# Token mixing of an encoder layer: two heads of a direction in one tile, gates first, a hand-written order of steps

## The chip, the cores and the metric

The kernel runs on one core of a Trainium2 chip. Its engines are PE (TensorE, matrix products; PEld is its weight load), DVE (VectorE), ACT (ScalarE), POOL (GpSimd) and SP (SyncE, which issues the loads here). Each takes its own instructions in order and waits for the others through semaphores. The metric is the device time of one execution in microseconds (us); lower is better.

## What is computed

```python
def rms_norm(x, g):
    return x * rsqrt(mean(x * x, -1) + EPS) * g

def swiglu(h, w_gate, w_up, w_down):
    return (silu(h @ w_gate) * (h @ w_up)) @ w_down

def gla_chunked(q, k, v, g):              # a head: dk 64, dv 128; 8 chunks of 64 tokens
    bcum = cumsum(g within the chunk);  b_last = its last row
    q_in, k_in = q * exp(bcum), k * exp(-bcum)
    att = tril(q_in @ k_in.T);  o_intra = att @ v
    k_st = k * exp(b_last - bcum);  d_state = k_st.T @ v
    state[n + 1] = exp(b_last[n]) * state[n] + d_state[n]
    return o_intra + q_in @ state

def token_mixing(h):                      # q k v r z_fwd z_bwd | Bg Cg xv = h @ w_in
    g = log_sigmoid(z @ w2 + b2) / 16     # per direction, rank 16
    o = gla(q / 8, k, v, g_fwd) + flip(gla(flip(q / 8), flip(k), flip(v), flip(g_bwd)))
    a = rms_norm(o per head, gla_norm) * silu(r)
    c = Bg * conv3(Cg * xv)
    return concat([a, c]) @ w_out

x = x + 0.5 * swiglu(rms_norm(x, ffn1_norm), ...)
x = x + token_mixing(rms_norm(x, mix_norm))
x = x + cross_attention(rms_norm(x, xattn_norm), rms_norm(mem, mem_norm))   # 4 heads, 256 memory tokens
x = x + 0.5 * swiglu(rms_norm(x, ffn2_norm), ...)
out = rms_norm(x, final_norm)             # 512 tokens, model width 1024, feed-forward width 2816
```

All is float32. The kernel makes each large product out of three products of a rounded part and a remainder.

## The kernel before

Activations lie transposed, 128 channels on the partitions and 512 tokens on the free axis; `x` and its two parts `xs` have eight such tiles. A weight unit is a slab of 128 x 1024 that SP loads into `raw` (L59), ACT rounds into `whi` (L65) and DVE completes with `wlo`, the remainder (L66). `mm3` (L68 to L73) makes three products of it on PE: whi with the high part of x (L69), whi with the low part (L70), wlo with the high part (L71). A unit of columns is 24 such products of 512 columns (`mm_cols`). Four raw buffers and three each of whi and wlo are in flight.

Four stages follow each other: the first feed-forward half step, token mixing, cross attention, the second half step with the last norm. The stage that changes is token mixing. The Tile framework orders the instructions of each engine by the code, its priorities and a cost model; on the chip every engine's order is then fixed. Small products that belong to sums over tokens wait in a list (`pend`) and go in one at a time after each `mm3` (`tick`).

Token mixing of before goes like this. `vps` takes v in two parts, part 0 (256 columns) and then part 1 (256 columns of v, and the 32 of z); the norm's factor goes to the tokens (`tok`) and, by `spread` (L145), to rows. `qk` projects q and k, 128 channels for two heads at a time, and copies each head's 64 rows to both halves of a tile (L410, L411): a head's tile has the forward direction in rows 0 to 63 and the backward one in rows 64 to 127. The gates come after q: four products of z, then log-sigmoid by `Abs`, `Exp`, `Ln` on ACT with `mn` on DVE and a subtraction on POOL (L443). `gate(h)` sums them per chunk by two scans of 64 x 512, one per direction (L449, L450), and makes `kin`, `qin`, `kst` and the decay.

`gla(h)` is a head in five steps: (1) four transposes of kst into `tp`, copied to `kn` by ACT (L482); (2) 16 products `dS` and 12 updates of the state S on DVE (L506, L508), a direction at a time in 64 rows; (3) eight products `ap`, and `att` made from them by two masked copies `put` and an addition `both` (L518, L524); (4) `ops`, four products with att and eight with S and qin, and o, its squares `osq` (L537, L539); (5) sums of the squares `rt_o`, and `spread`, which gives the head's output its factor (L545). `spread` makes two diagonal tiles `dg` on DVE (L162) and two products `sp_o` with ones on PE (L164). `rstd_tok` has the 1/rms: `ms` on DVE (L138), the root on POOL (L139). `gla_out` takes silu(r) on POOL.

Round the heads stand the units of the convolution, of `silu_r` and of the memory. `conv(j)` has three units, c, x and b (`cps`, `xps`, `bps`). The memory is split with its gain (`mem_split`), its squares are added on POOL (`mssq`), its factor is spread as `sp_mem` and multiplied into each key tile when it leaves PSUM; `mem_keys` has eight units (`mkps`), `mem_values` eight more. The order of these is a planner's: `skewed` starts a head four steps after the one before, and a loop over the units takes one step of a head after each unit.

## Time and profile before

| | before |
|---|---|
| time, median of 3 runs | 1152.45 us (1152.05 to 1152.57) |
| the profiled execution, its span | 1150.4 us |
| PE busy, of the span | 1118.1 us, 97% |
| DVE, ACT, POOL busy | 50%, 34%, 15% |
| token mixing, 370.77 to 618.29 | 247.52 us, PE busy 226.83 |
| granted clock of PE in it | 0.94 |

The profile is one execution of the program. Busy time counts matrix products on PE; register and semaphore instructions and the issue of loads don't count. The granted clock is a share of full speed. In a timeline row the first number is the start in us from the start of the span, the second the time that the instruction (or the xN merged ones) took, then engine, line, operation, output<-inputs and shape; in brackets is the idle time before it and what ended it.

### The profile page before, as it was taken

How to read it: one execution, taken by the hardware profiler on the slowest of the kernel's cores; microseconds unless marked ns; L12 is line 12 of the kernel's file. 1: busy time of each engine (PE TensorE's matmuls, PEld its weight loads, DVE VectorE, ACT ScalarE, POOL GpSimd, SP SyncE). 2: the span in 40 equal slices, each digit the busy share in tenths (PEclk: the TensorE clock that was granted, in tenths of full speed). 3: DMA queues.
4: the chain of work that ended last, by engine and by line, in shares of the span. 5: the costliest groups of instructions: out<-in, count | busy, mean ns of one | idle time of the engine just before them, and what ended most of it. 6: DMA issues, size and time to landing. Idle time of an engine off the chain costs nothing.

```text
span 1150.4 us, 13140 instructions
## 1 busy us (share of the span) xinstructions
PE 1118.1 (97%) x5326; PEld 934.3 (81%) x5326; DVE 576.9 (50%) x735; ACT 392.0 (34%) x549; POOL 173.9 (15%) x145
## 2 busy tenths in 40 slices
PE   8999999999999997798999999999999999999997
PEld 6888888888888986687887888888888888888886
DVE  6455455442333459855767445464555455442223
ACT  6332332322223284322334344353332332232221
POOL 4111111010111027211111300031111011000110
PEclk9999999999999999999999999999999999999998
DMA  6322222323333312311333322032222322323312
GB/s 218 113 95 98 100 92 94 106 85 101 101 95 124 109 56 64 101 56 57 128 104 117 105 79 74 19 128 92 92 92 93 109 92 92 105 83 101 101 51 74
DMA packets 34252, 109.08 MB, mean 95 GB/s; under 512 B 4080, under 2 KB 7152, under 8 KB 34192
## 3 DMA queue, kind: packets, MB, share of 16 engines
q1 hardware_dynamic: 34048, 108.23, 28.8%
q8 instruction: 41, 0.67, 0.2%
q14 instruction: 19, 0.16, 0.0%
q10 hardware_dynamic: 144, 0.02, 0.0%
HBM read 106.14 MB, written 2.10 MB: 94 GB/s over the span
## 4 chain that ended last, share of the span: by engine, by line
PE 86%; DVE 7%; issue 3%; ACT 1%; POOL 1%; DMA 1%; SPq 0%; POOLq 0%; DVEq 0%; ACTq 0%
PE pg_b L69 4%; PE pg_b L71 3%; PE pd_a L69 3%; PE pu_b L71 3%; PE pu_b L69 3%; PE pg_b L70 3%; PE pd_a L71 3%; PE pd_a L70 3%; PE pu_b L70 3%; PE pu_a L71 3%; PE pu_a L70 3%; PE pu_a L69 3%; PE pg_a L69 3%; PE pg_a L70 3%; PE pg_a L71 3%
## 5 line engine op out<-in xcount | busy, mean ns | idle before, releaser
L71 PE MATMUL pu_a<-xh,wlo_ua 128*128 128x512 f32 x176 | 68.7, 390 | 1.3 <-DVE wlo_ua L66 1.3
L71 PE MATMUL pg_a<-xh,wlo_ga 128*128 128x512 f32 x176 | 68.7, 391 | 0.6 <-DVE wlo_ga L66 0.6
L69 PE MATMUL pg_a<-xh,whi_ga 128*128 128x512 f32 x176 | 69.2, 395 | 0.0
L70 PE MATMUL pg_a<-xl,whi_ga 128*128 128x512 f32 x176 | 68.9, 392 | 0.1
L69 PE MATMUL pg_b<-xh,whi_gb 128*128 128x512 f32 x176 | 68.8, 391 | 0.0
L69 PE MATMUL pu_a<-xh,whi_ua 128*128 128x512 f32 x176 | 68.6, 390 | 0.0
L70 PE MATMUL pg_b<-xl,whi_gb 128*128 128x512 f32 x176 | 68.5, 389 | 0.0
L70 PE MATMUL pu_a<-xl,whi_ua 128*128 128x512 f32 x176 | 68.5, 389 | 0.0
L71 PE MATMUL pg_b<-xh,wlo_gb 128*128 128x512 f32 x176 | 68.5, 389 | 0.0
L71 PE MATMUL pu_b<-xh,wlo_ub 128*128 128x512 f32 x176 | 68.5, 389 | 0.0
L69 PE MATMUL pd_a<-hh_a,whi_da 128*128 128x512 f32 x176 | 68.5, 389 | 0.0
L70 PE MATMUL pd_a<-hl_a,whi_da 128*128 128x512 f32 x176 | 68.5, 389 | 0.0
L71 PE MATMUL pd_a<-hh_a,wlo_da 128*128 128x512 f32 x176 | 68.5, 389 | 0.0
L69 PE MATMUL pu_b<-xh,whi_ub 128*128 128x512 f32 x176 | 68.5, 389 | 0.0
L70 PE MATMUL pu_b<-xl,whi_ub 128*128 128x512 f32 x176 | 68.5, 389 | 0.0
L69 PE MATMUL pd_b<-hh_b,whi_db 128*128 128x512 f32 x154 | 59.9, 389 | 0.0
L70 PE MATMUL pd_b<-hl_b,whi_db 128*128 128x512 f32 x154 | 59.9, 389 | 0.0
L71 PE MATMUL pd_b<-hh_b,wlo_db 128*128 128x512 f32 x154 | 59.9, 389 | 0.0
L235 POOL TENSOR_TENSOR fh_a<-fs_a,fb_a 128x512 f32<-128x512 f32 x22 | 30.8, 1402 | 186.5 <-DVE fb_a L233 155.6
L235 POOL TENSOR_TENSOR fh_b<-fs_b,fb_b 128x512 f32<-128x512 f32 x22 | 28.4, 1292 | 198.9 <-DVE fb_b L233 182.2
L66 DVE TENSOR_TENSOR wlo_db<-raw_db,whi_db 128x896 fp32r<-128x896 f32 (+1 forms) x24 | 29.3, 1220 | 54.8 <-ACT whi_db L65 54.2
L66 DVE TENSOR_TENSOR wlo_da<-raw_da,whi_da 128x896 fp32r<-128x896 f32 (+1 forms) x24 | 28.4, 1182 | 49.8 <-ACT whi_da L65 49.1
(361 smaller groups left out, 2773.3 us busy)
## 6 DMA issues: line engine op xcount, KB each, us to landing
raw_gb<-in_w2gu SPq DMA_DIRECT2D x22, 512.0 KB, 3.5
raw_ub<-in_w2gu SPq DMA_DIRECT2D x22, 512.0 KB, 3.4
raw_ga<-in_w1gu SPq DMA_DIRECT2D x21, 512.0 KB, 3.5
raw_ua<-in_w1gu SPq DMA_DIRECT2D x21, 512.0 KB, 3.4
raw_da<-in_w1d SPq DMA_DIRECT2D x16, 448.0 KB, 3.3
raw_db<-in_w2d SPq DMA_DIRECT2D x16, 448.0 KB, 3.2
raw_da<-in_w1d SPq DMA_DIRECT2D x8, 512.0 KB, 3.5
raw_wk<-in_wk SPq DMA_DIRECT2D x8, 512.0 KB, 3.6
```

The lines of the kernel that those rows point to most:

```text
L66: nc.vector.tensor_tensor(lo[:, c], raw[:, c], hi[:, c].bitcast(F32), ALU.subtract)
L69: nc.tensor.matmul(ps, lhsT=whi, rhs=xhi, start=start, stop=False)
L70: nc.tensor.matmul(ps, lhsT=whi, rhs=xlo, start=False, stop=False)
L71: nc.tensor.matmul(ps, lhsT=wlo, rhs=xhi, start=False, stop=stop)
L235: nc.gpsimd.tensor_tensor(h, s, b, ALU.mult)
```

## The change

Two heads of one direction now share a tile of 128 rows: rows 0 to 63 belong to head 2j, rows 64 to 127 to head 2j + 1, and the tiles are named (r, j) for direction r and pair j. A projection of q or k leaves PSUM as it is, without copies. A scan, a state update, a subtraction now work on 128 rows of one direction: four scans of 128 x 512 in place of eight of 64 x 512, 24 updates of 128 x 128 in place of 48 of 64 x 128. The products of a head can't be shared: dS has 16 for a tile, each with weights of 64 rows and 64 columns, S has 32 for a pair, each with 64 rows.

The order of the first part is: v part 1 with z, q0, q1 with the gates in the middle, k0, k1, the gate of tile (0, 0), v part 0, the gate of (1, 0). The subtraction after `Ln` and the product with kst go to DVE, that of qin to POOL. The convolution's factor goes to cv on POOL before the last unit. The memory's squares come as four tiles of 512 columns added on DVE; its factor is spread before the splits and multiplied in with the gain, so that keys and values leave PSUM by a split alone. The steps of `gla(0)` and `gla(1)`, the convolutions, r and the keys are called one after another in a list written out by hand.

```diff
+    gbias = const.tile([P, 2 * NP], F32, name="gbias")
+    for r in DIRS:
+        for hh in range(2):
+            nc.sync.dma_start(gbias[hh * 64:(hh + 1) * 64, r * NP:(r + 1) * NP],
+                              t["headc"][r * 64:(r + 1) * 64, hh:H:2])
     gatew = big("gatew")[0:32, :]
-    nc.sync.dma_start(gatew, t["gatew"])
+    for r in DIRS:
+        nc.sync.dma_start(gatew[:, r * NP * P:(r + 1) * NP * P].rearrange("p (h c) -> p h c", c=64),
+                          t["gatew"].rearrange("p (h r c) -> p r h c", r=2, c=64)[:, r])
...
+    vz(1, 4, nmix.tok)
+    rtok = nmix.r
...
+    def qk(dst, key, j, sc, between=None):
+        ps = bank(f"{key}ps{j}")
+        w = unit(win[key][j], D, f"w{key}{j}")
+        mm_cols(ps, w, xs, ALL[:4], True, False)
+        if between:
+            between()
+        mm_cols(ps, w, xs, ALL[4:], False, True)
+        nc.vector.scalar_tensor_tensor(dst[j], ps, sc, rstd, ALU.mult, ALU.mult)
...
+    GT = [(r, j) for j in range(NP) for r in DIRS]
+    lgs, ts, lns = {}, {}, []
+    def gates():
+        for r, j in GT:
+            ps = bank(f"gps{r}{j}")
+            n = r * NP + j
+            c = slice(n * P, (n + 1) * P)
+            mm3(ps, gh[:, c], gl[:, c], zh, zl, True, True)
...
+        for g in GT:
+            nc.vector.tensor_tensor(lgs[g], lgs[g], ts[g], ALU.subtract)
...
+    qk(q2, "q", 0, 0.125, turn_z)
+    qk(q2, "q", 1, 0.125, gates)
+    qin, kin, kst, dec = {}, {}, {}, {}
+    def gate(r, j):
+        bc, lg = ts[r, j], lgs[r, j]
+        if r == 0:
+            nc.vector.tensor_tensor_scan(bc, rst[0], lg, 0.0, ALU.mult, ALU.add)
+        else:
+            nc.vector.tensor_tensor_scan(bc[:, ::-1], rst[1][:, ::-1], lg[:, ::-1], 0.0, ALU.mult, ALU.add)
...
+        nc.vector.tensor_tensor(lg, k2[j], lg, ALU.mult)
+        kst[r, j] = lg
+        nc.gpsimd.tensor_tensor(bc, k2[j], bc, ALU.mult)
+        kin[r, j] = bc
+        nc.gpsimd.tensor_tensor(e1, q2[j], e1, ALU.mult)
+        qin[r, j] = e1
...
+    qk(k2, "k", 0, 1.0)
+    qk(k2, "k", 1, 1.0)
+    gate(0, 0)
+    vz(0)
...
+    gate(1, 0)
...
-        s = tmp.tile([P, T], F32, tag="fb", name=f"{key}s{j}")
-        nc.vector.scalar_tensor_tensor(s, ps, sc, rstd, ALU.mult, ALU.mult)
-        for hh in range(2):
-            src = s[hh * 64:(hh + 1) * 64, :]
-            nc.scalar.copy(dst[2 * j + hh][0:64, :], src)
-            nc.scalar.copy(dst[2 * j + hh][64:128, :], src)
...
-        nc.gpsimd.tensor_tensor(lgs[h], lgs[h], ts[h], ALU.subtract)
...
-        nc.gpsimd.tensor_tensor(df, k2[h], df, ALU.mult)
-        kst.append(df)
-        nc.vector.tensor_tensor(q2[h], q2[h], e1, ALU.mult)
-        qin.append(q2[h])
-        nc.gpsimd.tensor_tensor(k2[h], k2[h], bc, ALU.mult)
...
-        for n in range(NCH):
-            r = slice((n % 2) * 64, (n % 2) * 64 + 64)
-            nc.tensor.matmul(dS[n % 2][:, (n // 2) * P:(n // 2 + 1) * P],
-                             lhsT=kn[r, (n // 2) * P:(n // 2 + 1) * P], rhs=v[n // 2][r, h * P:(h + 1) * P],
-                             start=(n < 2), stop=(n >= NCH - 2), skip_group_check=True)
...
-        for s in range(1, NCH - 1):
-            nc.vector.scalar_tensor_tensor(S(FW, s + 1), S(FW, s), dec[h][FW, s:s + 1], ds(FW, s), ALU.mult, ALU.add)
-            n = NCH - 1 - s
-            nc.vector.scalar_tensor_tensor(S(BW, n - 1), S(BW, n), dec[h][BW, n:n + 1], ds(BW, n), ALU.mult, ALU.add)
...
+            order = list(range(NCH)) if r == 0 else list(range(NCH))[::-1]
...
+            for n in order:
+                tk = ROWS[n % 2]
+                for hh in range(2):
+                    h = 2 * j + hh
+                    nc.tensor.matmul(dS[n % 2][ROWS[hh], (n // 2) * P:(n // 2 + 1) * P],
+                                     lhsT=kn[tk, (n // 2) * P + hh * 64:(n // 2) * P + (hh + 1) * 64],
+                                     rhs=v[n // 2][tk, h * P:(h + 1) * P],
+                                     start=n in order[:2], stop=n in order[-2:], skip_group_check=True)
...
+            for a, b in zip(order[1:], order[2:]):
+                nc.vector.scalar_tensor_tensor(S(r, full, b), S(r, full, a), dec[r, j][:, a:a + 1], ds(a),
+                                               ALU.mult, ALU.add)
...
-            nc.tensor.matmul(ops[:, c], lhsT=S(slice(0, P), n), rhs=qin[h][:, c],
-                             start=False, stop=(n == NCH - 1), skip_group_check=True)
...
+            for r in DIRS:
+                for hh in range(2):
+                    nc.tensor.matmul(ops[hh][:, c], lhsT=S(r, ROWS[hh], n), rhs=qin[r, j][ROWS[hh], c],
+                                     start=False, stop=(n == NCH - 1 and r == 1), skip_group_check=True)
...
+            nc.gpsimd.tensor_tensor(os[hh], os[hh], sr[2 * j + hh], ALU.mult)
+        for hh in range(2):
+            h = 2 * j + hh
+            ps = spread(rs[hh], 4, f"o{h}")
+            nc.vector.scalar_tensor_tensor(os[hh], os[hh], headc[:, H + h:H + h + 1], ps, ALU.mult, ALU.mult)
+            ah, al = big(f"ah{h}", F32R), big(f"al{h}", F32R)
+            split(os[hh], ah, al)
...
+        nc.gpsimd.tensor_tensor(cv, cv, rstd, ALU.mult)
...
-        nc.gpsimd.tensor_tensor(cv, bs, cv, ALU.mult)
+        nc.vector.tensor_tensor(bs, bps, cv, ALU.mult)
...
+    def mem_squares():
+        mssq = big("mssq")
+        nc.scalar.activation(mssq, mraw[0], AF.Square)
+        for i in range(1, KD // 2):
+            sq = tmp.tile([P, T], F32, tag="sq", name=f"msq{i}", bufs=2)
+            nc.scalar.activation(sq, mraw[i], AF.Square)
+            nc.vector.tensor_tensor(mssq, mssq, sq, ALU.add)
+        r_, todo = rstd_tok([mssq[:, 0:NM], mssq[:, NM:2 * NM]], 2, D, "mem")
+        for part in todo:
+            pend.extend(part)
+        mem["r"] = r_
+    def mem_rows():
+        mem["rows"] = big("mr")[:, 0:NM]
+        nc.scalar.copy(mem["rows"], spread(mem["r"], 2, "mem"))
...
+        f = tmp.tile([P, T], F32, tag="fa", name=f"mf{d}")[:, 0:NM]
+        nc.vector.scalar_tensor_tensor(f, raw, gains[:, GMEM, d:d + 1], mem["rows"], ALU.mult, ALU.mult)
+        m2 = big(f"mem{d}", F32R)
+        split(f, m2[:, 0:NM], m2[:, NM:2 * NM])
...
-            nc.vector.tensor_tensor(kf, ps[:, 0:NM], mr, ALU.mult)
             m2 = big(f"mk{n}", F32R)
-            split(kf, m2[:, 0:NM], m2[:, NM:2 * NM])
+            evict_split(ps[:, 0:NM], m2[:, 0:NM], m2[:, NM:2 * NM])
...
-    steps = skewed([gla(h) for h in range(H)], 4)
-    convs = chain(conv(j) for j in range(4))
-    for d in range(4):
-        next(convs)
-        gate(d)
-        mem_split(d)
...
+    g0, g1 = gla(0), gla(1)
+    cv = chain(conv(j) for j in range(4))
+    rr, kk = silu_r(), mem_keys()
+    next(cv)
+    next(g0)
+    next(cv)
+    next(g0)
+    gate(0, 1)
+    next(g0)
+    next(cv)
+    next(g0)
+    gate(1, 1)
+    next(cv)
+    next(g0)
+    mem_squares()
+    next(cv)
+    next(g0)
+    mem_rows()
+    next(cv)
+    for h in range(H):
+        next(rr)
+        if h == 0:
+            next(g1)
+        if h == 1:
+            next(g1)
+            next(g1)
+        if h == 2:
+            next(g1)
+        mem_split(2 * h)
+        mem_split(2 * h + 1)
+    next(g0)
+    next(kk)
+    next(g1)
+    next(kk)
+    next(g0)
+    next(g0)
+    next(kk)
+    next(g1)
+    next(cv)
+    next(g1)
+    next(cv)
+    next(cv)
+    next(g1)
+    next(g1)
+    for _ in cv:
         pass
-    for h in range(ndone, H):
-        gla_out(h)
+    for _ in kk:
+        pass
+    for _ in mem_values():
+        pass
```

On PE, the first dS block of before: each product has 128 columns of weights for a head of both directions, and neighbouring products read different halves of the rows (the two banks dS_3394 and dS_3395).

```order
L496 MATMUL dS_3394<-v_2849,kn_3342 128x128
L496 MATMUL dS_3395<-v_2849,kn_3342 128x128
L496 MATMUL dS_3394<-v_2850,kn_3342 128x128
L496 MATMUL dS_3395<-v_2850,kn_3342 128x128
L496 MATMUL dS_3394<-v_2851,kn_3342 128x128
L496 MATMUL dS_3395<-v_2851,kn_3342 128x128
```

And of after, tile (0, 0): x2 are the two heads of a chunk, 64 x 64 weights each.

```order
L511 MATMUL dS_3167<-v_2733,kn_3124 64x128 x2
L511 MATMUL dS_3168<-v_2733,kn_3124 64x128 x2
L511 MATMUL dS_3167<-v_2734,kn_3124 64x128 x2
L511 MATMUL dS_3168<-v_2734,kn_3124 64x128 x2
L511 MATMUL dS_3167<-v_2735,kn_3124 64x128 x2
L511 MATMUL dS_3168<-v_2735,kn_3124 64x128 x2
```

Where a head's chunk gave one product of 128 columns, two of 64 now follow each other on the same 64 rows of kn and v.

PE at the first spread of a head's output, before; xps and bps are convolution units.

```order
L70 MATMUL xps_3630<-xl_126,whi_wx_3632 128x512
L71 MATMUL xps_3630<-xh_125,wlo_wx_3633 128x512
L164 MATMUL sp_o_3667<-dg_o_3672,onesr 128x512
L164 MATMUL sp_o_3667<-dg_o_3675,onesr 128x512
L69 MATMUL bps_3679<-xh_111,whi_wb_3681 128x512
L70 MATMUL bps_3679<-xl_112,whi_wb_3681 128x512
```

And after; mkps are units of the memory's keys, sp_o_3883 and sp_o_3899 the factors of heads 0 and 1.

```order
L70 MATMUL mkps_3843<-mem_3760,whi_wk_3845 128x256
L71 MATMUL mkps_3843<-mem_3760,wlo_wk_3846 128x256
L164 MATMUL sp_o_3883<-dg_o_3888,onesr 128x512
L164 MATMUL sp_o_3883<-dg_o_3891,onesr 128x512
L164 MATMUL sp_o_3899<-dg_o_3904,onesr 128x512
L164 MATMUL sp_o_3899<-dg_o_3907,onesr 128x512
L69 MATMUL mkps_3915<-mem_3560,whi_wk_3917 128x256
L70 MATMUL mkps_3915<-mem_3560,whi_wk_3917 128x256
```

Two spreads now follow one another, with no unit between them.

DVE at that place, before: the work for sp_o_3667 with what stands ahead of it.

```order
L580 TENSOR_TENSOR bs_3568<-bps_3537,rstd_nmix 128x512
L66 TENSOR_TENSOR wlo_wb_3682<-raw_wb_3680,whi_wb_3681 128x1024
L120 TENSOR_TENSOR cl_3572<-cv_3510,ch_3571 128x512
L138 TENSOR_SCALAR ms_o_3603<-rt_o_3575 128x4
L158 CAST rh_o_3668<-r_o_3576 128x4
L159 TENSOR_TENSOR rl_o_3669<-r_o_3576,rh_o_3668 128x4
L162 TENSOR_TENSOR dg_o_3672<-ident,rh_o_3668 128x512
L162 TENSOR_TENSOR dg_o_3675<-ident,rl_o_3669 128x512
```

DVE after, from the output that needs sp_o_3883 to the second diagonal tile of sp_o_3899.

```order
L582 SCALAR_TENSOR_TENSOR o_3457<-o_3457,headc,sp_o_3883 128x512
L66 TENSOR_TENSOR wlo_wx_4039<-raw_wx_4037,whi_wx_4038 128x1024
L539 COPY_PREDICATED att_3837<-mf,both_3840 128x512
L648 TENSOR_TENSOR mk_3878<-mkps_3843,mk_3878 128x256
L120 TENSOR_TENSOR al_3896<-o_3457,ah_3895 128x512
L158 CAST rh_o_3900<-r_o_3766 128x4
L159 TENSOR_TENSOR rl_o_3901<-r_o_3766,rh_o_3900 128x4
L162 TENSOR_TENSOR dg_o_3904<-ident,rh_o_3900 128x512
L162 TENSOR_TENSOR dg_o_3907<-ident,rl_o_3901 128x512
```

Before, the rounding and both diagonal tiles stood behind one split of weights and one remainder; after, the second spread's stand behind an output that itself waits for the first spread, a split of weights, a masked copy and two remainders.

DVE at the sums of the memory's squares, after (before, they were POOL's).

```order
L596 TENSOR_TENSOR cs_3321<-cps_3290,rstd_3084 128x512
L66 TENSOR_TENSOR wlo_wr_3516<-raw_wr_3514,whi_wr_3515 128x1024
L539 COPY_PREDICATED att_3343<-mb,ap_3324 128x512
L545 TENSOR_TENSOR both_3346<-ap_3323,att_3343 128x512
L539 COPY_PREDICATED att_3349<-mb,ap_3326 128x512
L539 COPY_PREDICATED att_3343<-mf,both_3346 128x512
L545 TENSOR_TENSOR both_3352<-ap_3325,att_3349 128x512
L626 TENSOR_TENSOR mssq<-mssq,msq_3357 128x512
L539 COPY_PREDICATED att_3349<-mf,both_3352 128x512
L626 TENSOR_TENSOR mssq<-mssq,msq_3360 128x512
L626 TENSOR_TENSOR mssq<-mssq,msq_3363 128x512
```

The last of the three additions to mssq stands behind the four masked copies and the two additions of the first pair.

## Rows read from the trace of the kernel before

**Rows 1.** The page, part 1: span, and busy time of each engine.

```profile
span 1150.4 us, 13140 instructions
PE 1118.1 (97%) x5326; PEld 934.3 (81%) x5326; DVE 576.9 (50%) x735; ACT 392.0 (34%) x549; POOL 173.9 (15%) x145
```

**Rows 2.** Windows: length, busy PE, PEld, DVE, ACT, POOL, clock, DMA, GB/s.

```profile
370.77:618.29 247.52, 226.83 (x1272) 194.06 (x1271) 161.34 (x249) 95.87 (x141) 52.33 (x45) 0.94 0.27 86
```

**Rows 3.** Timeline of PE, token mixing: waits.

```profile
450.47 0.79 PE L71 MATMUL xps<-xh,wlo_wx 128*128 128x512 f32 x1 [3.58 <-DVE wlo_wx L66]
...
465.15 1.16 PE L496 MATMUL dS<-v,kn 64*128 64x128 f32 x16 [1.75 <-ACT kn L482]
...
484.54 2.04 PE L530 MATMUL ops<-att,v 128*128 128x128 f32 x8 [5.54 <-DVE att L518]
...
527.02 0.38 PE L164 MATMUL sp_mem<-dg_mem,onesr 128*128 128x256 f32 x1 [2.84 <-DVE dg_mem L162]
...
570.12 0.55 PE L530 MATMUL ops<-att,v 128*128 128x128 f32 x1 [2.73 <-DVE att L518]
...
616.84 0.47 PE L164 MATMUL sp_o<-dg_o,onesr 128*128 128x512 f32 x1 [0.72 <-DVE dg_o L162]
```

**Rows 4.** Windows with the lower clock (columns as in rows 2).

```profile
450.04:453.45 3.41, 2.98 (x7) 2.40 (x8) 3.35 (x4) 0.21 (x1) 1.51 (x1) 0.50 0.49 153
484.17:494.41 10.24, 9.87 (x35) 8.92 (x36) 4.42 (x7) 1.81 (x3) 0.00 (x0) 0.50 0.20 68
528.55:531.96 3.41, 3.15 (x9) 2.03 (x8) 2.33 (x4) 0.37 (x1) 0.70 (x1) 0.50 0.50 154
569.51:579.75 10.24, 9.63 (x45) 9.66 (x46) 3.26 (x6) 1.10 (x3) 0.00 (x0) 0.50 0.34 104
```

**Rows 5.** Timeline of PE at full clock: small products between large ones.

```profile
472.16 1.16 PE L514 MATMUL ap<-q,k 64*128 64x128 f32 x16
473.25 0.50 PE L69 MATMUL xps<-xh,whi_wx 128*128 128x512 f32 x1
473.59 0.39 PE L70 MATMUL xps<-xl,whi_wx 128*128 128x512 f32 x1
473.82 0.40 PE L71 MATMUL xps<-xh,wlo_wx 128*128 128x512 f32 x1
...
535.70 1.90 PE L534 MATMUL ops<-q,S 128*128 128x64 f32 x16
537.41 0.48 PE L69 MATMUL rps<-xh,whi_wr 128*128 128x512 f32 x1
```

**Rows 6.** Timeline of DVE, the gate stretch.

```profile
424.08 2.30 DVE L449 TENSOR_TENSOR_SCAN ta<-rst,mn 64x512 f32<-64x512 f32 x1 [5.00 <-POOL mn L443]
...
431.65 1.22 DVE L449 TENSOR_TENSOR_SCAN ta<-rst,mn 64x512 f32<-64x512 f32 x1
...
437.90 2.14 DVE L66 TENSOR_TENSOR wlo_wc<-raw_wc,whi_wc 128x1024 fp32r<-128x1024 f32 x1
```

**Rows 7.** Timelines of ACT and POOL, the gate stretch.

```profile
410.55 0.62 ACT L411 COPY q<-qs 64x512 f32<-64x512 f32 x1
...
411.90 1.28 ACT L436 ACT_TABLE_LOAD   x1
...
422.76 6.90 POOL L443 TENSOR_TENSOR mn<-mn,ta 128x512 f32<-128x512 f32 x4 [36.63 <-ACT ta L438]
```

**Rows 8.** Timeline of DVE: splits, masked copies, and a spread.

```profile
480.79 1.22 DVE L66 TENSOR_TENSOR wlo_wc<-raw_wc,whi_wc 128x1024 fp32r<-128x1024 f32 x1
481.92 0.72 DVE L518 COPY_PREDICATED att<-mb,ap 128x512 f32<-128x512 int32 x1
482.67 0.69 DVE L524 TENSOR_TENSOR both<-ap,att 128x512 f32<-128x512 f32 x1
...
614.44 0.16 DVE L138 TENSOR_SCALAR ms_o<-rt_o 128x4 f32<-128x4 f32 x1 [1.18 <-PE rt_o L133]
615.73 0.17 DVE L158 CAST rh_o<-r_o 128x4 fp32r<-128x4 f32 x1 [1.13 <-POOL r_o L139]
```

More of the change, by code (lines that the diff above doesn't have):

```diff
@@ L522, in gla @@
[L522 to L531 removed]
+            for r in DIRS:
+                for hh in range(2):
+                    nc.tensor.matmul(aps[hh][r][:, c], lhsT=kin[r, j][ROWS[hh], c], rhs=qin[r, j][ROWS[hh], c],
+                                     start=(i == 0), stop=(i == 3), skip_group_check=True)
```

288 lines of the change are left out of this document (119 added, 169 removed).

## The prediction, made before the changed kernel ran

> **What bounds the kernel now.** I read the busy shares first: PE is busy for 97% of the span [rows 1], so only three things can move the time: PE's idle time, the clock it is granted, and the number and price of its instructions. The change touches token mixing alone, so the second view is that stage cut out of the span: 247.52 us long, PE busy in 226.83 of them, clock 0.94 [rows 2]. PE thus stands idle for 247.52 - 226.83 = 20.7 us. The third view is PE's timeline, in which an idle time stands in brackets with what ended it. The reader is to see that PE always waits for a short chain on DVE or ACT: 3.58 us for the low half of a weight unit, 1.75 for kn, 5.54 and 2.73 for att, 2.84 for the diagonal tile of the memory's factor [rows 3]. After such a wait PE often runs on at half the clock (0.50, the lower of its two levels, 1.2 GHz): 3.41 us of it after the waits of 3.58 and 2.84, 10.24 us after those of 5.54 and 2.73 [rows 3, 4]. In these four stretches PE is busy for 2.98 + 9.87 + 3.15 + 9.63 = 25.6 us; at the full clock that is half, so the low clock costs 12.8 us. A perfect stage would win 20.7 + 12.8 = 33.5 us.
>
> **The change, part by part.** The account of time is that of the profiled execution: 1150.4 us of span, and the median of the runs shown is 2.1 us longer, which I add at the end.
>
> *The gate stretch.* Before, PE waits for weights because DVE is late: its first scan starts at 424.08 after an idle 5.00 us [rows 6], behind four subtractions on POOL that take 6.90 us [rows 7]; then eight scans, 1.22 us each alone and 2.30 beside POOL, and a weight split stretched to 2.14 us, stand before the units that PE wants [rows 6]. The change orders v with z first, makes the gates during q1, and gives the subtractions to DVE. Between the gates and the first convolution unit PE now has k0, k1 and the other part of v: 24 + 24 products of 0.23 us (473.59 to 473.82) [rows 5] and 96 half as wide, an estimate of 22.4 us. Walking the stage from 370.8 with these prices, the gate products end near 395.7. ACT then needs two table loads of 1.28 and, up to the first logarithm, six operations of about 0.62 [rows 7]: 402.9 with a little queueing. From there to the weights of the first convolution unit DVE has four subtractions, q and k of a pair, a weight split, four scans, small copies, three more operations of 512 columns, and the split itself; 512 columns take 0.69 and a split 1.22, and each overlaps the next by 0.08 (480.79 to 481.92) [rows 8]: 2.4 + 1.2 + 1.1 + 4.6 + 0.5 + 1.8 + 1.1 = 12.7, so 415.6, and PE wants them at 421.0. The next split follows 4.8 later, at 420.4, wanted at 426.9. POOL works beside it for four multiplications, which is 6.9 us by the like count of rows 7; if DVE runs at 1.22/2.14 of its pace for all of that [rows 6, 8], it loses 3.0. The slack of 5.4 and 6.5 covers it. So the waits for weights and for kn go (a unit of 24 products now lies between the transposes and dS); if the cover fails, PE waits 3 us or so and the clock falls.
>
> *Waits for att and for the memory's factor.* ops of the first pair now come a whole convolution unit after ap, 24 x 0.23 = 5.5 us, and those of the second pair after three key units; the memory's factor is spread well before its use. All the old waits are taken away: **-20.7**, and their low clock **-12.8**.
>
> *New waits.* (1) The row sums of the memory's squares stand behind DVE's work on att: from the end of unit c1, DVE does cs, one weight split, four masked copies (0.72 less the overlap), two additions (0.69) [rows 8] and three additions of squares, 0.2 + 0.6 + 1.1 + 2.6 + 1.2 + 1.8 = 7.5, while PE has ap and x1, 1.1 + 5.5 = 6.6. PE waits **1.0** (0.6 to 1.5). (2) Two spreads in a row, before mkps_3915. Before, each spread stood alone and cost at most 0.72 [rows 3]. Now the second one's diagonal tile is made behind everything in DVE's excerpt. From the end of the last r unit DVE has eight operations of 0.60, four masked copies of 0.65, three weight splits of 1.13, six of 256 columns (0.38, an estimate), some tiny ones, and the 1.3 us between ms_o at 614.44 and rh_o at 615.73, in which POOL takes the root [rows 8]: 4.8 + 2.6 + 3.4 + 2.3 + 0.5 + 1.3 = 14.9. PE meanwhile has two key units, the 16 ap products and the first spread: 5.8 + 1.1 + 0.5, some 1.5 for switches between kinds of products and small sums, and some 2 because the last key tile of memory is only split 4.8 after the start: 11.0. It waits 3.9, and 0.5 more for the second tile: **4.4**. The weight split standing among these rows waits for nothing; queued behind the wait on DVE is only the next head's output. (3) The last spread pair: the second diagonal tile comes behind bs, o (which waits for the first spread), a weight split and cl. From the end of the bps unit: 0.2 + 0.6 + 0.6 + 1.1 + 0.6 + 0.6 = 3.7, plus 0.2 until PE sees it, less the 0.5 of the first spread: **3.4**. Together 8.8; for the range 6 to 11, since neighbours on DVE's queue can shift by one or two operations.
>
> *Clock after them.* A wait of 2.84 was followed by 3.41 us at half clock, one of 2.73 by 10.24 [rows 3, 4]; that costs 3.0/2 = 1.5 or 9.8/2 = 4.9. I cannot tell which, and take the middle for both: **+6.4** (from 0 to 9.8).
>
> *Work on PE.* dS becomes 128 products instead of 64, each with 64 rows and 64 columns of weights; the trace shows none such. The nearest is ap, 64 rows by 128 columns in alternating row groups: 16 in 1.09 us (472.16 to 473.25), 0.068 each [rows 5]. If the two heads' products lie fully side by side, the 128 take the time of the old 64: +0. If each goes alone at the price of S, 16 in 1.71 (535.70 to 537.41), 0.107 [rows 5], it is 13.7 - 4.4 = +9.3. I take 0.068, as the form is nearest to ap: +4.4. S becomes 128 of 64 rows in alternating groups instead of 64 of 128 rows (6.8 us): between +0 and 128 x 0.107 - 6.8 = +6.9; at ap's 0.068 it is 8.7, +1.9. Two more sums for the memory, 0.1. Work: **+6.4** (0 to 16.3). In the new dS order the two heads of one chunk, issued next to each other, use the same 64 rows, and only chunks alternate. The Trainium skill, TensorE: Matmul & The Clock Gate, Part 3: Packing small matmuls, says that a weight load overlaps a running product only where the row group differs; by it half of the dS products would cost 0.107, 64 x 0.039 = 2.5 us more, 1143.1 in all. The ap rows, where groups alternate each time, can't decide that.
>
> *At nothing:* the 16 copies that leave ACT (ACT is half idle in the stage); fewer scans and state updates on DVE beyond what the walk counts; normalizing the memory first and evicting directly; the convolution's product shifted to DVE, hidden behind the next unit's 5.5 us; the added small loads of gate biases at the start. Were DVE short again, they would show in the waits above.
>
> **Sum:** -20.7 - 12.8 + 8.8 + 6.4 + 6.4 = -11.9. Span 1150.4 - 11.9 = 1138.5, time 1138.5 + 2.1 = 1140.6.
>
> **The rivals.** *Better:* the half clock doesn't follow the new waits as long (-4), and dS and S cost little (-5): about 1131. For it: in the stage the wait of 1.75 shows no fall, so short waits may be free [rows 3, 4]. Against it: 2.73 and 2.84 did bring one.
> *DVE late in the gate stretch:* POOL's multiplications slow the scans as before, the slack is eaten, PE waits 3 and runs slow for 1.5: about 1145. For it: 2.30 against 1.22 for a scan [rows 6]. Against: a slack of 5.4 and more.
> *The packed products go one after another:* dS and S at 0.107, +16.2 instead of +6.3: 1150.5, within 0.2% of before. For it: 64 x 64 is a form that the trace doesn't have. Against: ap runs 64-row products in pairs already.
> *Slower:* each of these products also pays for a switch. After ap the first large product takes 0.34 (473.25 to 473.59) where others take 0.23 [rows 5], 0.11 for a change of form; if two neighbours on different parts of the array pay it between them, a product costs 0.107 + 0.05 = 0.157, and 256 of them 256 x (0.157 - 0.068) = 22.8 more: 1163.4. It decides from 0.068 + 14.2/256 = 0.123 each. Against: ap changes groups at every product and pays nothing. The Trainium skill, TensorEngine Tiling (Array Packing), Key Properties, says that a change of tiling mode drains the engine and a change of tile alone does not; by that this rival is wrong inside a block, and ap agrees.
> *It doesn't do what it says:* the order brings a wait as long as those removed at another place, 1152.
>
> **How the numbers follow.** Forecast, 1134 to 1147: 0.55. Better: 0.21. DVE late: 0.09. Packed one by one: 0.07. Slower: 0.05. Nothing gained: 0.03. The likeliest is 1140.6. The range is 1129 (no half clock and cheap products, 1140.6 - 6.4 - 5) to 1150.5 (the serial case); outside it lie the slower case, the case of nothing gained, and half of the serial one and some of the better one, under 0.2. A measurement of this kernel can tell about 0.2%, 2.3 us, from no change. Faster by more: 0.55 + 0.21 + 0.09 + a little of the serial case = 0.87. Same: 0.07. Slower: 0.06.
>
> **What would show it.** In the profile after: PE idle in the stage of some 9 us instead of 20.7; no wait for wlo of the convolution or for att; waits of 3 to 5 us before the second of two neighbouring spreads; clock above 0.94; 16 dS products of 64 x 64 in about 1.1 us, S likewise 32 in 2.2. I am wrong if PE waits for weights between k1 and x1, if these blocks take over 1.7 and 3.4, or if the double spreads find their tiles ready.

## The result, and the profile after

The changed kernel takes 1132.11 us (median of 4 runs, 1128.61 to 1134.76) where the old one takes 1152.25 (4 runs, 1150.21 to 1152.57). The ratio is 0.984, with a 95% interval of 0.981 to 0.987: 20 us less, where 12 were forecast. The profiled execution is the shortest of the four, 1128.61 us with a span of 1126.9.

The page of the changed kernel, part 1, answers [rows 1]:

```profile
span 1126.9 us, 13354 instructions
PE 1105.8 (98%) x5458; PEld 926.3 (82%) x5458; DVE 552.6 (49%) x702; ACT 381.4 (34%) x529; POOL 158.5 (14%) x131
```

The windows of the changed kernel by stage, columns as in [rows 2]: the first half step, token mixing, and the rest.

```profile
0.00:370.29 370.29, 367.08 (x1614) 302.37 (x1615) 167.61 (x170) 119.50 (x156) 55.12 (x54) 1.00 0.36 110
370.29:595.55 225.26, 216.21 (x1405) 186.58 (x1404) 142.45 (x223) 87.27 (x124) 38.60 (x31) 0.98 0.30 94
595.55:1126.90 531.35, 522.51 (x2441) 437.35 (x2439) 242.56 (x310) 174.59 (x250) 64.82 (x46) 0.99 0.28 89
```

Token mixing went from 247.52 to 225.26 us. PE's idle time in it is 225.26 - 216.21 = 9.05 us instead of 20.69, and its busy time fell by 10.6 although some 130 instructions were added. PE's waits over the whole span (engine and line, what was waited for, us in total, times, the longest):

```profile
PE sp_o L164 <- DVE dg_o L162: 8.5, 2, 5.0
...
PE rt_mem L133 <- DVE mssq L626: 0.5, 1, 0.5
```

These are all of token mixing's waits; the others in that view lie at the start and in the last norm. Those for weights, kn, att and the memory's factor [rows 3] are gone. PE's timeline shows the remaining waits in their places, with the new blocks of small products:

```profile
432.78 1.10 PE L511 MATMUL dS<-v,kn 64*64 64x128 f32 x32
433.81 0.66 PE L499 MATMUL tp<-ident,mn 128*128 128x128 f32 x4
...
454.88 1.02 PE L133 MATMUL rt_mem<-ones,mssq 128*128 128x1 f32 x8 [0.53 <-DVE mssq L626]
...
457.72 3.79 PE L560 MATMUL ops<-e,S 64*128 64x64 f32 x64
461.44 0.51 PE L164 MATMUL sp_mem<-dg_mem,onesr 128*128 128x256 f32 x2
...
508.94 1.40 PE L164 MATMUL sp_o<-dg_o,onesr 128*128 128x512 f32 x2 [5.05 <-DVE dg_o L162]
...
542.48 0.47 PE L164 MATMUL sp_o<-dg_o,onesr 128*128 128x512 f32 x1 [3.47 <-DVE dg_o L162]
```

A dS block of 32 products lasts from 432.78 to 433.81, 1.03 us or 0.032 for each product, where 0.068 was taken; 64 S products last from 457.72 to 461.44, 3.72 or 0.058 each. (The trace has two records for each of these small f32 products of the program, 128 for the 64 of dS; the counts and prices of the prediction and of what follows are those of records.) The clock after the two long waits, by windows:

```profile
506.50:513.30 6.80, 4.36 (x17) 3.95 (x18) 4.39 (x9) 0.63 (x1) 0.00 (x0) 0.50 0.24 77
542.50:553.00 10.50, 10.50 (x46) 8.70 (x47) 4.39 (x6) 1.69 (x2) 0.00 (x0) 1.00 0.23 70
```

Behind the wait of 5.05 PE works 4.36 us at half the clock, which costs 2.2; behind that of 3.47 the clock didn't fall in this execution.

### The profile page after: what moved, and what is told of

It reads as the page before. It is cut to its first block, busy times and chain, and to the rows that moved or that the text cites. A ratio compares the mean times of both kernels' runs of the same rounds, so it can differ in the third digit from the quotient of the medians.

```text
span 1126.9 us, 13354 instructions
## 1 busy us (share of the span) xinstructions
PE 1105.8 (98%) x5458; PEld 926.3 (82%) x5458; DVE 552.6 (49%) x702; ACT 381.4 (34%) x529; POOL 158.5 (14%) x131
## 4 chain that ended last, share of the span: by engine, by line
PE 95%; DVE 2%; issue 1%; DMA 1%; ACT 0%; SPq 0%; POOLq 0%; POOL 0%; DVEq 0%; ACTq 0%
PE pg_b L69 4%; PE pg_b L71 4%; PE pu_b L71 4%; PE pd_a L70 4%; PE pd_a L71 4%; PE pg_b L70 4%; PE pu_b L70 4%; PE pu_b L69 4%; PE pd_a L69 4%; PE pu_a L71 3%; PE pu_a L69 3%; PE pu_a L70 3%; PE pg_a L70 3%; PE pg_a L71 3%; PE pg_a L69 3%; PE pd_b L70 3%
## 5 line engine op out<-in xcount | busy, mean ns | idle before, releaser
L66 DVE TENSOR_TENSOR wlo_gb<-raw_gb,whi_gb 128x1024 fp32r<-128x1024 f32 x22 | 46.6, 2120 | 12.8 <-ACT whi_gb L65 12.8
```

The costliest lines, as they stand in the source:

```text
L66: nc.vector.tensor_tensor(lo[:, c], raw[:, c], hi[:, c].bitcast(F32), ALU.subtract)
```

## The experiments

"Both apart" is the kernel of the third experiment; those after it are built on it, but for the fourth (on the changed kernel) and the ninth (on the old one). The old kernel was timed again beside each group: 1151.88 us beside experiments 1 to 4, 1147.84 beside 5 to 8, 1149.66 beside 9 and 10, 1147.62 beside 11 and 12. Both apart was timed beside the first group alone, so a difference of some 4 us between it and a later experiment is not shown by the times. There the profiled executions decide: their blocks, their waits and the length of their token mixing, which is 225.26 us in the changed kernel and 214.17 in both apart.

### The two waits, taken away one at a time

The first experiment puts two other pieces of work between the spreads of heads 0 and 1:

```diff
     next(g0)
-    next(g0)
     next(kk)
     next(g1)
+    next(g0)
     next(cv)
```

> The second spread of heads 0 and 1 moves behind one unit of keys and ops of the second pair; nothing else is moved. Theory (PE waits only for DVE's queue, 5.05 us at this place in the changed kernel): PE arrives some 5.7 us later, DVE's second diagonal tile comes 1.5 us later than now because one weight split and one key remainder slip ahead of it, so about 1 us of the wait stays; with the half clock behind it (3.4 us, worth 1.5) the profiled span falls by 5 to 6 us, from 1126.9 to about 1121.5. If the spread of the changed kernel's times (1128.6 and 1130.1 against 1134.2 and 1134.8) comes from the clock after this wait, the runs agree within 1 us; if it comes from the wait of heads 2 and 3, they still fall in two groups 4 to 5 us apart. Rival (DVE is simply short of time in this stretch): the wait comes back at the next product that needs DVE, and the time stays within 1.5 us.

Measured: 1124.43 us (1123.88 to 1125.43). The wait of 5.05 is gone altogether, not only down to 1; token mixing takes 219.30 us. The second wait is where it was, and this time the clock fell behind it:

```profile
536.37 0.77 PE L164 MATMUL sp_o<-dg_o,onesr 128*128 128x512 f32 x1 [3.47 <-DVE dg_o L162]
```

```profile
535.91:539.33 3.42, 2.96 (x7) 2.41 (x8) 1.52 (x3) 0.00 (x0) 0.00 (x0) 0.50 0.48 153
```

The second experiment does the same for heads 2 and 3:

```diff
     next(g1)
+    next(cv)
     next(g1)
     for _ in cv:
```

> The second spread of heads 2 and 3 moves behind the c unit of the last convolution (24 products, 5.5 us); the first pair stays as it is. Theory: the wait of 3.47 us goes, its diagonal tiles are ready before PE arrives; 3.5 us less, to about 1123.5 of span, where the clock didn't fall after this wait in the profiled run. If the two groups of times come from a fall of the clock after this wait (10.2 us at half clock cost 4.9), all runs now agree, and the median falls by 3.5 + 2.5 = 6; if they come from the first wait, two groups remain. Rival (DVE short of time): no change of over 1.5 us.

Measured: 1127.19 us (1125.88 to 1128.53); the wait of 3.47 is gone and the one of 5.06 stays, with the low clock behind it. The runs still spread over 2.6 us.

```profile
507.95:514.78 6.83, 5.21 (x21) 4.79 (x22) 3.58 (x8) 0.63 (x1) 0.00 (x0) 0.50 0.23 77
```

The third experiment makes both moves:

> Both moves. Theory: 8.5 us of waits fall to about 1, and no half clock is left in token mixing: stage 225.3 - 7.5 - 1.5 = about 216.3, span about 1118, time about 1119.5 to 1120, and the runs agree within 1 us. Rival: with the two waits gone DVE's queue makes PE wait elsewhere in the stage, by 3 us or more.

Measured: 1119.53 us (1118.52 to 1121.13), ratio to the old kernel 0.972 (0.971 to 0.974). The windows of its token mixing:

```profile
370.81:584.98 214.17, 213.65 (x1405) 184.97 (x1404) 142.56 (x223) 87.30 (x124) 39.08 (x31) 1.00 0.31 99
```

214.17 us, PE busy but for 0.52, the clock full. So DVE was not short of time: the work that made the second diagonal tile late only stood ahead of it, and the waits don't come back elsewhere. The medians add up. Leaving only the wait of 3.47 costs 1124.43 - 1119.53 = 4.9, leaving only that of 5.06 costs 7.7, leaving both (the changed kernel, from the first comparison) 1132.11 - 1119.53 = 12.6. Of these 8.5 are the waits, so the clock after them costs about 4.1 in a middling run: 1.4 after the wait of 3.47, 2.6 after that of 5.06. The two windows above agree: work of 2.96 and of 5.21 us at half the clock costs 1.5 and 2.6. This kernel beats both that were given.

### What took the old waits away

> The changed kernel with v part 0 ahead again of part 1, so that only k0 and k1 (10.9 us of products instead of 22.4) lie between the gates and the first convolution unit. Theory A (the new order of the first part is what took away the waits for weights): the cover falls from 22.4 to 10.9, DVE's chain to the split of the c unit takes 12.7, PE waits 2 to 6 us in the first convolution and runs slow after it: +5 to +11 us. Theory B (the waits went because DVE has less to do and in a better order, four scans of 128 rows, no subtraction on POOL; the framework also puts the split of the first c unit ahead of the gates' chain here): weights come in time, PE waits at most 1 us for kst, and the time is within 2 us of the changed kernel's.

```diff
-    vz(1, 4, nmix.tok)
+    vz(0, 4, nmix.tok)
     rtok = nmix.r
+    vz(1)
...
-    vz(0)
```

Measured: 1136.46 us (1134.28 to 1144.0), 4 us above the changed kernel. No wait for weights came back, as theory B said, but its 2 us did not hold. The backlog on DVE that the shorter cover leaves shows up at the memory's sums, as 2.05 us in place of 0.53: from the subtractions at 416.65 to those sums DVE stands idle once, for 0.70 us, where in the changed kernel it has idle times of 3.81, 1.39 and 1.48 us on the way. The clock then fell for long. PE's timeline, then a window of the profiled execution, which was the longest of the five:

```profile
458.12 1.11 PE L133 MATMUL rt_mem<-ones,mssq 128*128 128x1 f32 x5 [2.05 <-DVE mssq L625]
```

```profile
458.21:475.28 17.07, 17.07 (x100) 15.79 (x101) 6.24 (x11) 2.17 (x4) 2.66 (x3) 0.50 0.10 32
```

17.07 us of work at half the clock, 8.5 us lost, after one wait of 2.05. In this execution the two waits at the double spreads were followed by 6.83 us of low clock each, too.

The seventh experiment takes the lighter load away too: v part 0 first, the subtraction on POOL, each scan in two halves.

```diff
-            nc.vector.tensor_tensor(lgs[g], lgs[g], ts[g], ALU.subtract)
+            nc.gpsimd.tensor_tensor(lgs[g], lgs[g], ts[g], ALU.subtract)
...
-            nc.vector.tensor_tensor_scan(bc, rst[0], lg, 0.0, ALU.mult, ALU.add)
+            for hr in ROWS:
+                nc.vector.tensor_tensor_scan(bc[hr], rst[0][hr], lg[hr], 0.0, ALU.mult, ALU.add)
...
```

> On top of the kernel with both pairs apart: v part 0 ahead of part 1 again, the four subtractions back on POOL, and every scan cut into its two halves of 64 rows (eight scans as before the change), the rest as changed. Theory (the waits for weights and kn of the old kernel came from DVE's and POOL's load between the gates and the convolution, and the changed kernel needs either the lighter load or the longer cover): with both gone PE waits 2 to 4 us in the first convolution for the split of a unit or for kst, kn, and the half clock after it adds 1.5 to 8: 1123 to 1131. Rival (those waits came from the planner's order of steps alone): nothing beyond what putting v part 0 first does by itself, a wait of some 1.5 us more at the sums of the memory's squares.

Measured: 1128.47 us (1127.55 to 1131.95), 9 above both apart; token mixing takes 226.57 us. The timelines of DVE, PE and ACT in the first convolution:

```profile
419.10 4.47 DVE L458 TENSOR_TENSOR_SCAN ta<-rst,mn 64x512 f32<-64x512 f32 x2 [2.07 <-POOL mn L446]
423.59 2.14 DVE L461 TENSOR_TENSOR_SCAN ta<-rst,mn 64x512 f32<-64x512 f32 x1
```

```profile
431.26 0.66 PE L501 MATMUL tp<-ident,mn 128*128 128x128 f32 x4 [1.30 <-DVE mn L476]
443.93 1.34 PE L513 MATMUL dS<-v,kn 64*64 64x128 f32 x20 [6.54 <-ACT kn L503]
```

```profile
441.83 0.63 ACT L472 ACTIVATE mn<-mn 128x512 f32<-128x512 f32 x1 [3.23 <-DVE mn L465]
...
443.31 0.57 ACT L503 COPY kn<-tp 128x512 f32<-128x512 f32 x1
```

Waits of 1.30 for kst and 6.54 for kn: more than the 2 to 4 expected, by the mechanism expected. The first three half scans stretch to 2.14 and more beside POOL, and the late gate of a later tile reaches PE through kn: ACT's copy of kn stands behind an operation of that gate, before which ACT waits 3.23 us for DVE. With the old order of v alone (the fourth experiment) no such wait came. So the lighter load suffices without the longer cover, and with both gone the waits return. Whether the longer cover would suffice without the lighter load was not tried.

The ninth puts one part of the change alone into the old kernel:

```diff
-        nc.gpsimd.tensor_tensor(lgs[h], lgs[h], ts[h], ALU.subtract)
+        nc.vector.tensor_tensor(lgs[h], lgs[h], ts[h], ALU.subtract)
```

> The old kernel with one part of the change alone: the four subtractions after the logarithm on DVE instead of POOL. In the old kernel DVE idles 5.00 us for POOL's subtractions, and then scans at 2.30 us beside POOL. Theory (these two are what makes the weights late by 1.40 + 0.78 + 3.58 us in the first convolution): the subtractions cost 2.4 us on DVE, the idle time goes, and the scans run at 1.22; the first scan comes some 3 us later than before, the eighth earlier; the three waits shrink from 5.8 to 1 to 4 us, with the clock 2 to 6 us less time, 1146 to 1150. Rival (what counts is the number of scans and the place of the whole stretch, not POOL): the later first scan makes kst and kn late instead, waits for kn grow beyond 1.75, and the time is the same or up to 3 us longer.

Measured: ratio 0.999 (0.997 to 1.001, medians 1146.65 and 1149.66 of 10 and 13 runs), so no change that can be told. Its waits of PE:

```profile
PE ops L530 <- DVE att L518: 8.2, 3, 4.5
PE sp_mem L164 <- DVE dg_mem L162: 2.8, 1, 2.8
PE bps L71 <- DVE wlo_wb L66: 2.7, 1, 2.7
PE dS L496 <- ACT kn L482: 1.9, 1, 1.9
...
PE bps L69 <- ACT whi_wb L65: 1.1, 1, 1.1
```

The waits for weights moved to the next unit, b, and shrank from 5.8 to 4.4 us with a short one for x; the others stayed. Neither theory nor rival names this move to the next unit: POOL's subtraction is at most one of several causes, and moving it is not enough.

### Why att is no longer late

> On top of the kernel with both pairs apart: each of the 24 state updates of 128 rows is cut into two of 64 rows, 24 more instructions on DVE of about 0.36 us, 2.2 us in each of four bursts. Theory (DVE has idle time of 1.4 to 3.8 us behind each burst of the first pair, so the saved updates were not what took away the waits for att): the sums of the memory's squares come up to 1 us later and PE's wait there grows from 0.5 to about 1.5; time +0.5 to +3. Rival (the number of state updates decides the waits for att): waits for att or kn of 2.5 us and more come back, and the time rises by 4 or more.

```diff
-                nc.vector.scalar_tensor_tensor(S(r, full, b), S(r, full, a), dec[r, j][:, a:a + 1], ds(a),
-                                               ALU.mult, ALU.add)
+                for hr in ROWS:
+                    nc.vector.scalar_tensor_tensor(S(r, hr, b), S(r, hr, a), dec[r, j][hr, a:a + 1], ds(a)[hr],
+                                                   ALU.mult, ALU.add)
```

Measured: 1124.89 us (1123.94 to 1132.47), 5.4 above both apart; token mixing takes 220.35 us, 6.2 more. PE's timeline:

```profile
456.58 1.02 PE L133 MATMUL rt_mem<-ones,mssq 128*128 128x1 f32 x8 [1.72 <-DVE mssq L627]
...
497.35 0.39 PE L70 MATMUL mkps<-mem,whi_wk 128*128 128x256 f32 x1 [0.57 <-DVE mem L120]
```

The wait at the sums is as expected, 1.7. Not expected were waits of 1.0 and 0.6 for the key tiles of the memory and 6.8 us of half clock from 500 on. Of the 6.2 us the longer waits are 2.8 and the low clock 3.4. No wait for att came back, so the rival falls by its mechanism, though its 4 us came: the saved updates are worth 5 to 6 us here, at other places.

The eleventh puts the convolution's product back on POOL. In the old kernel DVE idled for it, ahead of the first head's state updates; DVE's timeline there:

```profile
473.87 0.69 DVE L120 TENSOR_TENSOR cl<-cv,ch 128x512 fp32r<-128x512 f32 x1 [1.83 <-ACT ch L119]
474.48 0.28 DVE L503 COPY S<-dS 64x128 f32<-64x128 f32 x1
```

```diff
-        nc.gpsimd.tensor_tensor(cv, cv, rstd, ALU.mult)
...
-        nc.vector.tensor_tensor(bs, bps, cv, ALU.mult)
+        nc.vector.tensor_tensor(bs, bps, rstd, ALU.mult)
+        nc.gpsimd.tensor_tensor(cv, bs, cv, ALU.mult)
...
```

> The kernel with both pairs apart, and the convolution's last product back on POOL as in the old kernel (DVE scales the unit, POOL multiplies, ACT rounds, DVE takes the remainder cl). In the old kernel DVE stands idle 1.83 us for this chain at 473.87, ahead of the state updates of the first head, and PE then waits 5.54 us for att. Theory A (that idle time, with what stands behind it, is what made att late; it is the convolution's new form that took the wait away): cl comes about 1 us later in the b unit of each convolution, DVE idles there, and PE waits 1.5 us or more longer at the sums of the memory's squares or at ops; +2 to +5. Theory B (in the new order DVE has idle time behind it, 1.5 us after the second tile's state updates): no wait grows by over 0.5 us, and the time stays within 1 us of 1119.5.

Measured: 1118.86 us (1117.75 to 1120.29); token mixing takes 214.16 us, PE busy in 213.64, and the only wait in it is the one at the memory's sums, 0.52. Theory B holds: in the new order this part of the change buys nothing.

The twelfth moves ops of the second pair close to ap:

```diff
     next(kk)
-    next(g0)
-    next(kk)
     next(g1)
     next(g0)
+    next(kk)
+    next(g0)
     next(cv)
```

> The kernel with both pairs apart, and ops of the second pair right after one unit of keys (2.9 us) behind ap instead of two units and a spread. Theory (the distance in PE's order between ap and ops hides the masked copies, 0.7 us each four times, with two additions and what stands between them): PE arrives at ops some 3 us after ap, the second att is ready about 5 us after it, so PE waits 1.5 to 2.5 us for att and the clock may fall after it: +1.5 to +5. Rival (att is never late in the new order, whatever the distance, since DVE has little else to do): no wait for att over 0.5 us, time within 1 us.

Measured: 1122.07 us (1121.95 to 1122.4), 2.5 more; token mixing takes 218.13 us, 3.96 more.

```profile
506.50 1.13 PE L554 MATMUL ops<-att,v 128*128 128x128 f32 x8 [0.81 <-DVE att L539]
507.56 1.10 PE L560 MATMUL ops<-e,S 64*128 64x64 f32 x8
508.59 1.16 PE L554 MATMUL ops<-att,v 128*128 128x128 f32 x8
```

A wait for att of 0.81 is back, half of what was expected. The rest of the 3.96 is no wait: 3.41 us of half clock between 396 and 402, before the place of the edit, are 1.7 of it. And the products of ops take 6.89 us, from 506.50 to 513.39, where they take 5.60 in both apart: PE's order changed with the edit, eight records of S now stand between the att products of the two heads and start one at a time, 0.112 us apart, and so do some of those behind; in both apart they start in pairs. So the distance in PE's order hides part of att's chain for the second pair. Which part of the change took away the 5.54 us at the first head was not isolated; none of the three parts tried here brings it back alone.

The tenth, with the memory's squares one unit earlier:

> The kernel with both pairs apart, and the memory's squares one unit earlier, ahead of the second tile's dS: their three additions then stand among the state updates, before the masked copies. Theory: the wait of 0.5 us at the sums goes, or turns into one of up to 0.8 at the new place and up to 0.5 for att; time 1119 to 1120.5, not to be told from 1119.5. Rival (the additions delay the state updates and with them ops): 1 us or more longer.

Measured: 1119.42 us (1118.69 to 1121.49); token mixing takes 214.25 us. A wait of 0.66 stands at the new place of the sums. Nothing gained.

### The price of the packed products

> On top of the kernel with both pairs apart (1119.5). In each dS block the eight products of one head come first, then the eight of the other; nothing else is moved. In the changed kernel the 128 products take 4.14 us, 0.032 each, where 0.068 was forecast. Theory: neighbours that lie on different quarters of the array (rows or columns) run side by side, and the old sequence goes round all four quarters. By head, neighbours still change rows but keep the columns, like ap, so the price goes to ap's 0.054 to 0.068: blocks of 16 take 0.9 to 1.1 instead of 0.52, all eight together 2.8 to 4.5 us more, time 1122 to 1124. Rival (only a change of rows lets a weight load overlap, columns don't matter): the new order alternates rows at every product and is as fast or faster: change of 0 or less. Rival (a 64 x 64 product is cheap however it is ordered): no change within 1 us.

```diff
-            for n in order:
-                tk = ROWS[n % 2]
-                for hh in range(2):
+            for hh in range(2):
+                for n in order:
+                    tk = ROWS[n % 2]
```

The first block of 32 products on PE, in both apart and then by head, each with what follows it:

```profile
433.30 1.10 PE L511 MATMUL dS<-v,kn 64*64 64x128 f32 x32
434.33 0.44 PE L499 MATMUL tp<-ident,mn 128*128 128x128 f32 x2
```

```profile
434.84 1.59 PE L511 MATMUL dS<-v,kn 64*64 64x128 f32 x32
436.37 0.33 PE L499 MATMUL tp<-ident,mn 128*128 128x128 f32 x1
```

1.03 us become 1.53, 0.032 each become 0.048, and the 128 take 6.1 instead of 4.1 us. The order matters, though less than the 2.8 to 4.5 us of the theory. The time of 1119.94 (1119.67 to 1121.42) can't tell 2 us; token mixing takes 217.64 us, 3.5 more than in both apart, of which 1.7 are a low clock ahead of the blocks (last section). The rival that only rows count falls: with rows changing at every product the block is slower than with a pair on the same rows and different columns. The rival that order doesn't count falls with it.

The starts of the records in the trace show what stands behind the prices. In both apart's dS block four records start within 0.02 us, one group of four every 0.109 us: as many as there are quarters of 64 rows and 64 columns in 128 x 128. By head two start together, every 0.109 us; only where the second head takes over do they come closer. The S records of the changed kernel start two at a time, every 0.112 us.

> On top of the kernel with both pairs apart. In ops all 16 S products of one head come first, then the 16 of the other, so that neighbours use the same 64 rows of the array; nothing else is moved. In the changed kernel the 128 take 7.4 us, 0.058 each. Theory (alternating rows are what makes them cheap): each goes alone at the price of the S products before, 0.107, the two blocks of 64 take 6.9 instead of 3.7 us, 6.3 us more in all, time about 1126. Rival (the price is set by something else, such as 64 columns with 64 rows): no change within 1 us.

```diff
-        for n in range(NCH):
-            c = slice(n * 64, (n + 1) * 64)
-            for r in DIRS:
-                for hh in range(2):
+        for hh in range(2):
+            for n in range(NCH):
+                c = slice(n * 64, (n + 1) * 64)
+                for r in DIRS:
```

Measured: 1133.67 us (1132.04 to 1134.57), 14 more where 6.3 were expected; token mixing takes 230.12 us, 16 more. PE's timeline and windows:

```profile
459.91 8.26 PE L560 MATMUL ops<-e,S 64*128 64x64 f32 x64
```

```profile
460.00:464.00 4.00, 4.00 (x40) 4.00 (x41) 2.60 (x5) 0.27 (x1) 1.52 (x2) 1.00 0.29 115
464.00:468.00 4.00, 4.00 (x26) 3.98 (x25) 0.69 (x1) 0.32 (x1) 0.00 (x0) 0.66 0.00 0
468.00:472.00 4.00, 4.00 (x11) 3.23 (x11) 0.69 (x1) 0.97 (x2) 0.00 (x0) 0.50 0.00 0
```

At full clock 40 products go in 4.00 us, 0.100 each, near the 0.107 of [rows 5], and they start one at a time, 0.112 us apart: alternating rows is what halves the price. (Neighbours on different rows also write different banks of PSUM, in every order tried here, so rows and banks are not told apart.) Then the clock falls while PE is busy in every microsecond: 6.8 us at half of it from within the first block on, and 10.2 from within the second. With 3.4 after the gate products (last section) that is 20.5 us of work, 10.2 lost. The theory had the price and missed the clock.

## Why the prediction was right in the whole, and where it was wrong

The measured 1132.11 us lies in the stated range, but outside the 1134 to 1147 that had the largest chance. What came is the case *Better* (about 1131, chance 0.21), with both of its conditions: the clock and the small products cost less than the sum took.

*The gate stretch: right, by its own steps.* DVE after the gates in the changed kernel:

```profile
403.39 2.50 DVE L444 TENSOR_TENSOR mn<-mn,ta 128x512 f32<-128x512 f32 x4 [1.29 <-ACT ta L439]
...
414.62 1.22 DVE L66 TENSOR_TENSOR wlo_wc<-raw_wc,whi_wc 128x1024 fp32r<-128x1024 f32 x1
...
420.68 2.20 DVE L66 TENSOR_TENSOR wlo_wx<-raw_wx,whi_wx 128x1024 fp32r<-128x1024 f32 x1
```

The logarithms are there at 403.39 (402.9 forecast), the first split ends at 415.8 (415.6), the second at 422.9 (420.4 forecast). It takes 2.20 us, and a small copy before it 1.29, while POOL works from 414.45 to 425.7, which is some 2.1 of the 3.0 us that the forecast allowed for POOL; the first split, with POOL at work too, takes its usual 1.22. Both lie within the slack: PE takes up the two low halves from 421.79 and from 427.70 on. The rival with DVE late did not come.

*The old waits: right.* All of them went. For the gate stretch DVE's lighter load is shown to suffice, and the waits return when load and cover are both undone (fourth and seventh experiment); that the longer cover alone would have done it, as the forecast's slack has it, was not tried. For att the share of each part is only argued. The fewer state updates, which the forecast put at nothing, are not nothing: without them both apart takes 5 to 6 us longer (eighth experiment).

*The new waits: right, 9.05 us for 8.8 forecast.* 0.53 for 1.0 at the memory's sums, 5.05 for 4.4 and 3.47 for 3.4 at the double spreads. DVE's timeline at the first double spread shows the rows that the forecast counted there:

```profile
504.60 0.73 DVE L582 SCALAR_TENSOR_TENSOR o<-o,headc,sp_o 128x512 f32<-128x512 f32 x1
505.26 1.21 DVE L66 TENSOR_TENSOR wlo_wx<-raw_wx,whi_wx 128x1024 fp32r<-128x1024 f32 x1
506.39 0.71 DVE L539 COPY_PREDICATED att<-mf,both 128x512 f32<-128x512 int32 x1
507.01 0.40 DVE L648 TENSOR_TENSOR mk<-mkps,mk 128x256 fp32r<-128x256 f32 x1
507.33 0.67 DVE L120 TENSOR_TENSOR al<-o,ah 128x512 fp32r<-128x512 f32 x1
507.93 0.15 DVE L158 CAST rh_o<-r_o 128x4 fp32r<-128x4 f32 x1
508.12 0.17 DVE L159 TENSOR_TENSOR rl_o<-r_o,rh_o 128x4 fp32r<-128x4 f32 x1
508.20 0.68 DVE L162 TENSOR_TENSOR dg_o<-ident,rh_o 128x512 fp32r<-128x512 f32 x1
```

From o at 504.60 on, 3.6 us of DVE's work stand ahead of the second spread's tile at 508.20; of this it needs only its own rounding, rh_o and rl_o. That the order is the cause, and not a shortage of DVE's time, is shown by the first three experiments.

*Clock after them: mechanism right, size off.* +6.4 was taken, the middle of two bounds because nothing told them apart; the profiled execution paid 2.2, and by the medians of the first three experiments a middling run pays 4.1. The two bounds, 0 and 9.8, held.

*Work on PE: the step that failed.* "I take 0.068, as the form is nearest to ap" was the wrong end. dS costs 4.1 us where 8.7 were taken: the low bound, fully side by side, four records at a time. S costs 7.4 where 8.7 were taken and 6.8 before. That the sum is near nothing can be read from the stage too: PE's busy time fell by 10.6 us, and the low clock accounts for 12.8 - 2.2 = 10.6 of that. The form nearest in rows was not nearest in price, because a 64 x 64 product leaves free columns beside it as well as rows: ap and S run two at a time, dS four. The fifth experiment shows 0.032 for neighbours in pairs on the same rows and 0.048 with rows alternating on the same columns; the sixth, where neighbours share rows and all columns, 0.100. The two rivals that made the products dear fall with the same rows, and a change of tile inside a block costs nothing to be seen.

The rule quoted in the prediction from the Trainium skill (TensorE: Matmul & The Clock Gate, Part 3: Packing small matmuls), that a weight load overlaps only where the row group differs, would have made dS dearer. Here the measurement, 0.032 against 0.048, decides against it as far as different columns go; the 0.100 of the sixth experiment agrees with it. The other page quoted there (the Trainium skill, TensorEngine Tiling (Array Packing), Key Properties), by which a change of tile alone does not drain the engine, agrees with the 0.032.

*The account.* Forecast span 1138.5; work -6.4, clock -4.2, waits +0.25, and 1.2 less outside the stage (370.29 + 531.35 against 370.77 + 532.11) give 1126.95; measured 1126.9. The median lies 3.5 above the profiled run's time, which goes with the clock of the runs: 0.994 and 0.994 in those of 1128.61 and 1130.06, 0.990 and 0.989 in those of 1134.15 and 1134.76.

## What to carry to other kernels

Where the bound engine waits for a short chain on another one, look at what stands ahead of that chain in the other engine's order rather than at its load: with two reorderings of steps and no work removed, 8.5 us of waits and the low clock behind them went, and nothing came back. A price for packed small products should be read by rows and by columns: in these runs neighbours that shared neither, or only one of them, ran side by side (0.032, 0.048 and 0.058 us each), and neighbours that shared both did not (0.100). And a part undone alone may bring no wait back where two undone together do, as the fourth and the seventh experiment show for the waits in the first convolution.

## What the hardware showed that was not expected

The granted clock does not fall after idle time alone. With S by head, it went from 1.00 to 0.50 (1.2 GHz) between 464 and 468 while PE was busy without a break, after more than 4 us of products that use 64 of the 128 rows one at a time; PE's last wait, 0.54 us, had ended at 457.06. In five of the twelve profiled executions (experiments 5, 6, 7, 9 and 12) it also stood at half for 3.41 us right after the gate products, which have 32 rows; PE was busy all the time. In the fifth, sixth and twelfth that is between 396 and 402. Here is the window of the fifth:

```profile
395.00:402.00 7.00, 7.00 (x25) 5.29 (x24) 2.25 (x3) 5.65 (x9) 0.00 (x0) 0.76 0.11 46
```

In the profiled executions of the changed kernel and of both apart, with the same products there, the clock stayed full. How long the lower clock stays varies as much: behind the same wait of 3.47 us it did not come in the changed kernel's profiled execution, stood for 3.4 us in the first experiment's and for 6.8 in the fourth's, where a wait of 2.05 was followed by 17.07. What decides it was not tried.
